# Last token tile: second norm and store moved between engines, six small tiles moved to another pool, a scratch tile shared

## The chip, the cores and the metric

The kernel runs on one core of one Trainium2 chip. The metric is the device time of one execution in microseconds (us); the number shown for a kernel is the median of its runs. The core has five engines that each work through a queue of their own in order: TensorE (PE in the rows, PEld for its weight loads), VectorE (DVE), ScalarE (ACT), GpSimd (POOL) and SyncE (SP). DMA transfers are issued from the queues of SyncE, ScalarE and GpSimd. A q behind an engine's name (SPq, ACTq) marks a row of its sequencer.

## The reference, cut to what matters

One transformer block on 2048 tokens of width 1024: a first norm with modulation, an input projection, three mixers (convolution, sparse attention, pooling), an output projection with a residual, a second norm with modulation, and a mixture of 32 experts with two experts for each token; at the end a norm over the rows. The change touches the seam between the output projection and the experts, and the last norm:

```python
x = x + g1 * mix
h = _rmsnorm(x, norm2_g[l]) * (1 + sc2) + sh2
x = x + g2 * _hier_moe(h, router_g_w[l], router_g_b[l], router_e_w[l], router_e_b[l],
                       exp_w1[l], exp_w3[l], exp_w2[l])
return _rmsnorm(x, final_g)
```

`_hier_moe` picks a group of experts by a softmax of four logits, then two of its eight experts, and adds the gated outputs of `(silu(h @ w1[e]) * (h @ w3[e])) @ w2[e]` to the tokens.

## The kernel before, in words

The kernel is written with tiles in pools; a scheduler puts the instructions of each engine's queue into a fixed order when the kernel is built, by program order and by a simulated time at which an instruction's inputs and its tile's memory are free. Pools that are open one after the other lie on the same memory, so a tile of a later pool waits until the last use of the tile of the earlier pool under it.

`output()` goes over 16 tiles of 128 tokens (`t` is 0 to 15). `product(t)` makes the output projection on TensorE, adds the residual on VectorE (`x`), takes the sum of squares on ScalarE (L1151 or L1156), stores `x` to `x1_d` from SyncE (L1157), and forms the reciprocal root `s` by VectorE and GpSimd (L99, L100). Then `h2 = x * s * A2 + B2` is formed and stored to `h2_d`, the rows that the experts gather. For tiles 0 to 14 that is two VectorE instructions (L1166, L1167) and a store by SyncE. For tile 15 (`last`) it is a ScalarE pass (L1160), four GpSimd passes of half a tile (L1163, L1164), and a store from ScalarE's queue (L1168).

`router(t)` transposes `x` and computes the 36 logits (L1181 to L1188). After every fourth tile `route()` turns the logits of four tiles into expert numbers, gates and positions, in a chain of some 50 small VectorE instructions (L1306 to L1395) with a few matmuls between them. The last `route()` also makes `en0`, the token list of the first expert (L1383, L1384). `order()` then counts the tokens of each expert and ranks the experts (L1422 to L1450); its small tiles `ex2`, `kc`, `kr`, `rank`, `gt`, `ov` are in `st`, the pool of `output()` that is given back at its end.

`moe()` works through 32 experts. Weights come by SyncE (`load`, L1712) into a ring of large tiles. `cut` splits them into a high part `wh` on ScalarE (L1728) and a low part `wl` on VectorE (L1729). For the first expert (`FIRST[0]`, 31) `gather` fetches the rows of `h2_d` on GpSimd by `en0` (L1646, tile `xg`); after that, `enter` writes the lists of the last four tiles by eight GpSimd scatters (L1406, `list_d<-enl,sil`). SyncE reads the list of the second expert from `list_d` (L1644) behind those, and GpSimd gathers by it (L1646, `ent`). `flip` transposes the gathered rows (L1674), `half1` makes the first two products with a tile `hr` for silu times gate (tag `hr`, 2 buffers, L1755 to L1757), `third` transposes `hr` (L1792) and makes the last product. `norm()` is the final norm of 128 rows: a square with a row sum on ScalarE whose output tile `jf` nobody reads (L1598), `rsqrt`, and a VectorE pass (L1600); it runs 22 times among and behind the last experts.

The places that fix the seam's order are these lines of `moe()`:

```python
prep(0)
with tc.issue_after(self.fetched.ins):
    self.enter(*self.late)
prep(1)
self.moe_tiles()
with tc.issue_after(self.listed.ins):
    self.flip(ex[0])
    self.half1(0, ex[0])
```

`fetched` is the gather of the first expert, `listed` the last VectorE copy into `en0`.

Of the kernel before, what the change touches and what calls it, by code (L numbers as in the profile page):

```python
# [10 lines left out]
F32 = mybir.dt.float32  # L11
F32R = mybir.dt.float32r
BF = mybir.dt.bfloat16
I16 = mybir.dt.int16
I32 = mybir.dt.int32
AF = mybir.ActivationFunctionType
OP = mybir.AluOpType
# [5 lines left out]
D = 1024  # L23
# [24 lines left out]
class K:  # L48
# [1040 lines left out]
    def output(self):  # L1089

        nc, a, tc = self.nc, self.a, self.tc
# [4 lines left out]
        with ExitStack() as c1:  # L1096
            wp = c1.enter_context(tc.tile_pool(name="ow", bufs=1, reuse_waits="tile"))
            st = c1.enter_context(tc.tile_pool(name="os", bufs=2, reuse_waits="tile"))
# [5 lines left out]
            with tc.issue_after(self.last.ins):  # L1104
                g1 = wp.tile([128, D], F32, name="g1")
                self.row(g1, 0)
                B2 = wp.tile([128, D], F32, name="B2")
                self.row(B2, 1)
                A2 = wp.tile([128, D], F32, name="A2")
# [22 lines left out]
            def product(t, mix):  # L1132
                mh, ml = mix
                ti = slice((t % 2) * 128, (t % 2) * 128 + 128)
                x = st.tile([128, D], F32, name="xr", tag="xr", bufs=3)
                nc.sync.dma_start(x, a["x"][0, t * 128:(t + 1) * 128, :])
                ps = self.big((128, 2, 512))
                last = t == NT - 1
                for m, k in ([(m, k) for m in range(2) for k in range(KT)] if last else
                             [(m, k) for k in range(KT) for m in range(2)]):  # L1140
                    s = slice(m * 512, (m + 1) * 512)
                    self.mm3(ps[:, m, :], mh[:, k, ti], ml[:, k, ti], W[k][0][:, s], W[k][1][:, s],
                             k == 0, k == KT - 1)
                h2 = st.tile([128, D], F32, name="h2", tag="h2", bufs=3)
                s = st.tile([128, 4], F32, name="s2", tag="s2", bufs=4)
                if last:
                    for m in range(2):
                        f = slice(m * 512, (m + 1) * 512)
                        nc.vector.tensor_tensor(h2[:, f], ps[:, m], g1[:, f], OP.mult)
                        nc.vector.tensor_tensor(x[:, f], x[:, f], h2[:, f], OP.add)  # L1150
                        nc.scalar.activation(h2[:, f], x[:, f], AF.Square, accum_out=s[:, 2 * m:2 * m + 1])  # L1151
                    nc.vector.tensor_tensor(s[:, 0:1], s[:, 0:1], s[:, 2:3], OP.add)
                else:
                    nc.vector.tensor_tensor(h2, ps.rearrange("p a b -> p (a b)"), g1, OP.mult)
                    nc.vector.tensor_tensor(x, x, h2, OP.add)
                    nc.scalar.activation(h2, x, AF.Square, accum_out=s[:, 0:1])  # L1156
                nc.sync.dma_start(self.x1_d[t * 128:(t + 1) * 128], x)  # L1157
                self.rsqrt(s[:, 3:4], s[:, 0:1], D, s[:, 1:2])
                if last:
                    nc.scalar.activation(h2, x, AF.Copy, scale=s[:, 3:4])  # L1160
                    for m in range(2):
                        f = slice(m * 512, (m + 1) * 512)
                        nc.gpsimd.tensor_tensor(h2[:, f], h2[:, f], A2[:, f], OP.mult)  # L1163
                        nc.gpsimd.tensor_tensor(h2[:, f], h2[:, f], B2[:, f], OP.add)  # L1164
                else:
                    nc.vector.scalar_tensor_tensor(h2, x, s[:, 3:4], A2, op0=OP.mult, op1=OP.mult)  # L1166
                    nc.vector.tensor_tensor(h2, h2, B2, OP.add)  # L1167
                (nc.scalar if last else nc.sync).dma_start(self.h2_d[t * 128:(t + 1) * 128], h2)  # L1168
                return x, s[:, 3:4]

            def router(t, x1):
# [19 lines left out]
            for t in range(NT):  # L1191
                i = t % 4
                h2 = product(t, mix)
                if t == 2:
                    self.rows, self.idle, self.held = None, 3 * ["S"] + self.LB * ["L"], {}
                    with tc.issue_after(self.last.ins):
                        self.early = [self.load13(self.expert(FIRST[0]), c) for c in range(2)]
                if t == 0:
                    self.route_consts(wp)
                    with tc.issue_after(self.last.ins):  # L1200
                        self.blank_lists(st)
                if prev is not None:
                    router(t - 1, prev)
                    c, _ = where[t - 1]
                    if where[t][0] > c:
                        self.route(c, lgs[c], st)
                if i % 2 == 0 and t + 2 < NT:
                    nxt = self.mixed(t // 2 + 1,
                                     [st.tile([128, KT, 256], F32R, name=n, tag=n, bufs=2) for n in ("mh", "ml")],
                                     [st.tile([128, 512], F32R, name="ol", tag="ol", bufs=4) for _ in range(2)],  # L1210
                                     st.tile([128, 4, 256], F32, name="yl", tag="yl", bufs=2),
                                     lambda: self.sm((128, 2, 256)))
                if i % 2:
                    mix = nxt
                prev = h2
            router(NT - 1, prev)
            c = len(self.GROUPS) - 1
            self.route(c, lgs[c], st)
            self.order(st)

    def mixed(self, c, mix, os_, y, bank):

# [187 lines left out]
                    self.tc.declare_no_dep(d.ins, o.ins, reason="each entry has its own slot")  # L1410
                self.scat.append(d)

    def order(self, st):

        nc = self.nc
        V = nc.vector
        ps = self.sm()
        tiles = [(c, i) for c in range(len(self.GROUPS)) for i in range(self.GROUPS[c])]
        for n, (c, i) in enumerate(tiles):
            O = self.O[c][:, i, :]  # L1420
            first, last = n == 0, n == NT - 1
            nc.tensor.matmul(ps[0:32, 0:32], self.onesb[:, 0:32], O, start=first, stop=False, skip_group_check=True)  # L1422
            nc.tensor.matmul(ps[0:32, 32:33], O, self.onesb[:, 0:1], start=False, stop=last, skip_group_check=True)

        ex = st.tile([32, 2], F32, name="ex2")
        V.tensor_copy(ex[:, 0:1], self.eid)
        V.tensor_copy(ex[:, 1:2], ps[0:32, 32:33])
        kc = st.tile([32, 1], F32, name="kc")
        V.tensor_scalar(kc, ex[:, 1:2], 32.0, self.eid, op0=OP.mult, op1=OP.subtract)
        kr = st.tile([32, 32], F32, name="kr")  # L1430
        V.scalar_tensor_tensor(kr, ps[0:32, 0:32], 32.0, self.e32[0:32], op0=OP.mult, op1=OP.subtract)
        for e, k in zip(FIRST, (-3e6, -1.5e6)):
            V.memset(kr[:, e:e + 1], k)
        V.tensor_scalar(kc, kc, self.bump, None, op0=OP.add)
        rank = st.tile([32, 1], F32, name="rank")
        V.tensor_scalar(kr, kr, kc, 0.0, op0=OP.is_gt, op1=OP.add, accum_out=rank)
        V.tensor_scalar(kr, self.e32[0:32], rank, None, op0=OP.is_equal)
        po = self.sm()
        for i in range(2):
            nc.tensor.matmul(po[0:1, i * 32:i * 32 + 32], ex[:, i:i + 1], kr, start=True, stop=True)  # L1440
        self.ordi = self.cst.tile([1, 32], I32, name="ordi")
        self.cnti = self.cst.tile([1, 32], I32, name="cnti")
        V.tensor_copy(self.ordi, po[0:1, 0:32])
        V.tensor_copy(self.cnti, po[0:1, 32:64])
        gt = st.tile([1, 32], F32, name="gt")
        V.tensor_tensor(gt, po[0:1, 32:64], self.capr, OP.is_gt)
        ov = st.tile([1, 1], F32, name="ov")
        V.tensor_reduce(ov, gt, axis=AX.X, op=OP.add)
        self.over = self.cst.tile([1, 1], I32, name="over")
        V.tensor_copy(self.over, ov)  # L1450
# [142 lines left out]

    def norm(self, x):
        n = x.shape[0]
        junk = self.mp.tile([128, D], BF, name="jf")
        s = self.mp.tile([128, 3], F32, name="sf", tag="sf", bufs=4)[:n]
        self.nc.scalar.activation(junk[:n], x, AF.Square, accum_out=s[:, 0:1])  # L1598
        self.rsqrt(s[:, 2:3], s[:, 0:1], D, s[:, 1:2], self.mhalf[:n])
        self.nc.vector.scalar_tensor_tensor(x, x, s[:, 2:3], self.fg[:n], op0=OP.mult, op1=OP.mult)  # L1600
# [296 lines left out]
```

## Time and profile before

| what | value |
|---|---|
| median of 3 runs | 2224.28 us (2223.84 to 2227.76) |
| the profiled execution, its own time | 2222.8 us |
| its span, first to last instruction | 2220.7 us |
| busy share of the span | PE 90%, DVE 71%, ACT 55%, POOL 40% |
| DMA over the span | 257 GB/s mean |

The profile is of one execution, which ran 1.5 us under the median; 2.1 us of it lie outside its span. Times in the rows count from the start of the span. A timeline row gives start, duration, engine, line, operation, output and inputs, how many instructions are merged in it, and in brackets the idle time of the engine ahead of it with what ended that wait.

### The profile page before, as it was taken

How to read it: one execution, taken by the hardware profiler on the slowest of the kernel's cores; microseconds unless marked ns; L12 is line 12 of the kernel's file. 1: busy time of each engine (PE TensorE's matmuls, PEld its weight loads, DVE VectorE, ACT ScalarE, POOL GpSimd, SP SyncE). 2: the span in 40 equal slices, each digit the busy share in tenths (PEclk: the TensorE clock that was granted, in tenths of full speed). 3: DMA queues.
4: the chain of work that ended last, by engine and by line, in shares of the span. 5: the costliest groups of instructions: out<-in, count | busy, mean ns of one | idle time of the engine just before them, and what ended most of it. 6: DMA issues, size and time to landing. Idle time of an engine off the chain costs nothing. (4 is left out here: it accounts for less than half of the span.)

```text
span 2220.7 us, 37647 instructions
## 1 busy us (share of the span) xinstructions
PE 2008.4 (90%) x12857; PEld 1512.5 (68%) x12858; DVE 1573.5 (71%) x3016; ACT 1215.7 (55%) x2027; POOL 885.2 (40%) x1599
## 2 busy tenths in 40 slices
PE   5899999988999999989889997799999999999983
PEld 4677887865667777767768886567777666666762
DVE  5596889668878888886446655667867666766673
ACT  4833333256778887777642222556666565665552
POOL 4442111546454333365000112445555455555443
PEclk9999999999999999999999998799999999999997
DMA  8736979869977666658867435799999899999884
GB/s 277 266 118 219 284 208 283 300 184 302 301 237 227 199 210 196 211 191 272 236 216 269 153 124 179 277 319 358 346 310 338 265 342 320 339 322 317 301 299 145
DMA packets 314388, 569.65 MB, mean 257 GB/s; under 512 B 36467, under 2 KB 149576, under 8 KB 313160
## 3 DMA queue, kind: packets, MB, share of 16 engines
q1 hardware_dynamic: 289560, 489.79, 65.8%
q0 software_dynamic: 22304, 68.41, 10.8%
q10 hardware_dynamic: 2320, 8.91, 1.0%
q8 instruction: 105, 1.72, 0.3%
q14 instruction: 99, 0.81, 0.1%
HBM read 462.44 MB, written 103.53 MB: 255 GB/s over the span
## 5 line engine op out<-in xcount | busy, mean ns | idle before, releaser
L1729 DVE TENSOR_TENSOR wl<-wr,wh 128x1024 fp32r<-128x1024 f32 x314 | 388.0, 1274 | 157.6 <-ACT wh L1728 156.5
L1728 ACT ACTIVATE wh<-wr 128x1024 fp32r<-128x1024 f32 x372 | 373.3, 1053 | 207.6 <-PE acc L94 166.5
L92 PE MATMUL acc<-wh,xh 128*128 128x512 f32 (+3 forms) x544 | 217.1, 409 | 7.2 <-ACT wh L1728 6.1
L93 PE MATMUL acc<-wl,xh 128*128 128x512 f32 (+3 forms) x544 | 219.5, 404 | 4.4 <-DVE wl L1729 4.3
L1026 DVE CUSTOM_DVE_ANT_0 L<-pl,bias 128x512 f32<-128x512 f32 (+3 forms) x312 | 180.5, 608 | 57.7 <-PE pt L1064 32.3
L94 PE MATMUL acc<-wh,xl 128*128 128x512 f32 (+3 forms) x544 | 215.7, 400 | 0.0
L1025 PE MATMUL pl<-kc,qa 128*128 128x512 f32 (+3 forms) x640 | 182.2, 390 | 14.3 <-DMA kc<-kh_d 7.3
L863 DVE SCALAR_TENSOR_TENSOR S<-rel,wi,S 128x512 f32<-128x512 f32 (+3 forms) x259 | 171.2, 683 | 30.7 <-ACT rel L862 30.1
L1066 ACT ACTIVATE pT<-pt 128x512 f32<-128x512 f32 (+1 forms) x288 | 158.7, 576 | 58.5 <-PE pt L1064 57.9
L1064 PE MATMUL pt<-identr,L 128*128 128x128 f32 x1088 | 170.9, 282 | 19.4 <-ACT pT L1066 13.7
L1729 POOL TENSOR_TENSOR wl<-wr,wh 128x1024 fp32r<-128x1024 f32 x58 | 145.2, 2563 | 105.2 <-ACT wh L1728 102.4
L862 ACT ACTIVATE rel<-pi 128x512 f32<-128x512 f32 (+3 forms) x296 | 154.2, 548 | 47.5 <-PE pi L860 28.5
L627 DVE SCALAR_TENSOR_TENSOR ac<-u,kc,ac 128x512 f32<-128x512 f32 x240 | 175.2, 774 | 0.1
L1064 PEld LDWEIGHTS pt<-identr,L 128*128 128x128 f32 x1088 | 126.0, 143 | 61.1 <-ACT pT L1066 22.6
L1031 ACT ACTIVATE L<-L,ast 128x128 f32<-128x128 f32 (+15 forms) x128 | 154.2, 1205 | 17.0 <-DVE ast L1030 16.8
L1051 PE MATMUL po<-pT,vc 128*64 128x128 f32 x2176 | 149.6, 283 | 9.6 <-ACT pT L1066 9.4
L1051 PEld LDWEIGHTS po<-pT,vc 128*64 128x64 f32 x2176 | 123.0, 140 | 41.4 <-ACT pT L1066 20.8
L859 PE MATMUL pi<-kk,qi 128*128 128x512 f32 (+3 forms) x296 | 128.5, 436 | 23.3 <-ACT rel L862 22.8
L1025 PEld LDWEIGHTS pl<-kc,qa 128*128 128x128 f32 x640 | 108.7, 193 | 42.3 <-DVE ast L1026 16.7
L92 PEld LDWEIGHTS acc<-wh,xh 128*128 128x128 f32 (+3 forms) x544 | 98.3, 183 | 43.4 <-ACT wh L1728 11.3
L93 PEld LDWEIGHTS acc<-wl,xh 128*128 128x128 f32 (+3 forms) x544 | 99.7, 183 | 38.3 <-issue 6.5
L1779 POOL DMA_INDIRECT x_d<-yo,ent x31 | 90.2, 2908 | 82.4 <-DVE yo L1822 57.1
(561 smaller groups left out, 4652.2 us busy)
## 6 DMA issues: line engine op xcount, KB each, us to landing
wr<-in_exp_w_dram SPq DMA_DIRECT2D x256, 512.0 KB
wr<-in_exp_w_dram SPq DMA_DIRECT2D x64, 1024.0 KB
h<-h_d SPq DMA_DIRECT2D x64, 512.0 KB
vc<-v_d SPq DMA_DIRECT2D x112, 256.0 KB
h_d<-h POOLq DMA_DIRECT2D x32, 512.0 KB, 6.0
qa<-qa_d SPq DMA_DIRECT2D x128, 128.0 KB
modr<-in_mod_w_dram SPq DMA_DIRECT2D x32, 512.0 KB
xt<-in_x_dram SPq DMA_DIRECT2D x16, 512.0 KB
```

The lines of the kernel that those rows point to most:

```text
L92: mm(out, lh, rh, start=start, stop=False)
L93: mm(out, lh, rl, start=False, stop=False)
L94: mm(out, ll, rh, start=False, stop=stop)
L627: nc.vector.scalar_tensor_tensor(acc[j], src, kc[:, j, i:i + 1], acc[j], op0=OP.mult, op1=OP.add)
L863: nc.vector.scalar_tensor_tensor(S[:, s:e], r[:, :e - s], self.wi[:, t, h:h + 1], S[:, s:e] if h else self.tie[:, s:e], op0=OP.mult, op1=O ...
L1025: nc.tensor.matmul(ps[:, :e - s], q[:, h % 2, m], k[:, s:e], start=m == 0, stop=m == 1)
L1026: nc.vector.tensor_tensor_reduce(L[:, s:e], ps[:, :e - s], bias[:, s:e], 1.0, -3e38, OP.add, OP.max, mx[:, i:i + 1])
L1051: nc.tensor.matmul(po[r], v[:, (k2 + i) % 4, r], pT[:, i, j], start=len(left) > 2 * t, stop=len(left) <= 2)
L1064: nc.tensor.transpose(pt[:, i, j], P[j][:, (k2 + i) * 128:(k2 + i + 1) * 128], self.ident)
L1066: nc.scalar.activation(pT[:, :m], pt[:, :m], AF.Copy)
L1728: nc.scalar.activation(H[:, s], W[:, s], AF.Copy)
L1729: (nc.gpsimd if pool else nc.vector).tensor_tensor(L[:, s], W[:, s], H[:, s].bitcast(F32), OP.subtract)
```

## The change

For tile 15 the second norm is done as for the other tiles: two VectorE instructions and a store by SyncE; ScalarE's pass, the four GpSimd passes and the store from ScalarE's queue go. The six small tiles of `order()` are taken from `cst`, the pool that stays open for the whole kernel. The scratch output of `norm()` takes a buffer of `hr` (same bytes) in place of one of its own.

```diff
                 self.rsqrt(s[:, 3:4], s[:, 0:1], D, s[:, 1:2])
-                if last:
-                    nc.scalar.activation(h2, x, AF.Copy, scale=s[:, 3:4])
-                    for m in range(2):
-                        f = slice(m * 512, (m + 1) * 512)
-                        nc.gpsimd.tensor_tensor(h2[:, f], h2[:, f], A2[:, f], OP.mult)
-                        nc.gpsimd.tensor_tensor(h2[:, f], h2[:, f], B2[:, f], OP.add)
-                else:
-                    nc.vector.scalar_tensor_tensor(h2, x, s[:, 3:4], A2, op0=OP.mult, op1=OP.mult)
-                    nc.vector.tensor_tensor(h2, h2, B2, OP.add)
-                (nc.scalar if last else nc.sync).dma_start(self.h2_d[t * 128:(t + 1) * 128], h2)
+                nc.vector.scalar_tensor_tensor(h2, x, s[:, 3:4], A2, op0=OP.mult, op1=OP.mult)
+                nc.vector.tensor_tensor(h2, h2, B2, OP.add)
+                nc.sync.dma_start(self.h2_d[t * 128:(t + 1) * 128], h2)
...
-            self.order(st)
+            self.order()
...
-        ex = st.tile([32, 2], F32, name="ex2")
+        ex = self.cst.tile([32, 2], F32, name="ex2")
...
-        kc = st.tile([32, 1], F32, name="kc")
+        kc = self.cst.tile([32, 1], F32, name="kc")
...
-        kr = st.tile([32, 32], F32, name="kr")
+        kr = self.cst.tile([32, 32], F32, name="kr")
...
-        rank = st.tile([32, 1], F32, name="rank")
+        rank = self.cst.tile([32, 1], F32, name="rank")
...
-        gt = st.tile([1, 32], F32, name="gt")
+        gt = self.cst.tile([1, 32], F32, name="gt")
...
-        ov = st.tile([1, 1], F32, name="ov")
+        ov = self.cst.tile([1, 1], F32, name="ov")
...
-        junk = self.mp.tile([128, D], BF, name="jf")
+        junk = self.mp.tile([128, D], BF, name="jf", tag="hr", bufs=2)
```

## Rows read from the trace of the kernel before

**Rows 1.** Stretches of 10 us: busy time by engine, granted clock, DMA share, GB/s.
```profile
1370.00:1380.00 10.00, 1.15 (x66) 0.71 (x64) 8.01 (x31) 2.79 (x7) 5.53 (x5) 0.76 1.04 410
...
1400.00:1410.00 10.00, 10.00 (x38) 7.62 (x37) 5.22 (x5) 5.62 (x6) 5.11 (x5) 0.87 0.04 2
1410.00:1420.00 10.00, 2.39 (x12) 2.17 (x12) 2.55 (x3) 3.39 (x5) 3.78 (x4) 0.64 0.91 331
```

**Rows 2.** Timeline of PE at the first two experts' transposes.
```profile
1395.96 1.25 PE L1674 MATMUL smm<-identr,xg 128*128 128x128 f32 x8 [8.27 <-DMA xg<-h_d,en]
...
1417.61 1.25 PE L1674 MATMUL smm<-identr,xg 128*128 128x128 f32 x8 [7.61 <-DMA xg<-h_d,ent]
```

**Rows 3.** Timeline of POOL through the seam.
```profile
1372.62 2.50 POOL L1163 TENSOR_TENSOR h<-h,A 128x512 f32<-128x512 f32 x2 [1.26 <-DMA wr<-in_exp_w_dram]
...
1388.32 1.05 POOL L1646 DMA_INDIRECT xg<-h_d,en  x1 [10.72 <-DVE ov L1448]
1389.68 6.50 POOL L1406 DMA_INDIRECT list_d<-enl,sil  x1 [0.30 <-issue]
...
1409.65 1.94 POOL L1646 DMA_INDIRECT xg<-h_d,ent  x1 [3.68 <-DMA ent<-list_d]
```

**Rows 4.** The eight scatters of L1406: ns min/median/max, first and last start; landing.
```profile
L1406 POOL DMA_INDIRECT list_d<-enl,sil x8: 965/970/6495, 1389.7 to 1404.1; - x8
...
DMA to landing us min/median/max: 2.1/2.7/10.2
```

**Rows 5.** Timeline of SP through the seam.
```profile
1380.56 0.34 SPq L1157 DMA_DIRECT2D x_d<-xr  x1
1387.55 3.26 SPq L1712 DMA_DIRECT2D wr<-in_exp_w_dram  x6
1407.13 0.94 SPq L1644 DMA_DIRECT2D ent<-list_d  x2
```

**Rows 6.** Waits of SP's queue, 1370 to 1420: total us, times, longest.
```profile
SPq L1644 <- DMA list_d<-enl,sil: 6.7, 1, 6.7
SPq L1712 <- DMA h_d<-h: 6.5, 1, 6.5
```

**Rows 7.** Timeline of DVE, last tile and order of the experts.
```profile
1371.89 0.25 DVE L1188 SCALAR_TENSOR_TENSOR lg<-sm,s,rb 128x36 f32<-128x36 f32 x1 [1.25 <-PE sm L1186]
...
1378.24 0.28 DVE L1343 TENSOR_TENSOR oe<-fo 128x128 f32<-128x128 f32 x1
...
1386.09 0.19 DVE L1383 TENSOR_SCALAR en<-have,spare 128x1 int32<-128x1 f32 x1
...
1388.41 6.88 DVE L1729 TENSOR_TENSOR wl<-wr,wh 128x1024 fp32r<-128x1024 f32 x6
```

**Rows 8.** Timeline of DVE, tile 3 and the first `route()`.
```profile
1215.81 1.29 DVE L1166 SCALAR_TENSOR_TENSOR h<-xr,s,A 128x1024 f32<-128x1024 f32 x1 [0.73 <-POOL s L100]
...
1221.59 0.28 DVE L1343 TENSOR_TENSOR oe<-fo 128x128 f32<-128x128 f32 x1
```

**Rows 9.** One line of `route()`, its four calls: ns min/median/max, first and last.
```profile
L1334 DVE TENSOR_TENSOR te<-lg,fo x4: 274/278/1306, 1219.6 to 1374.0; 128x128 f32<-128x128 f32 x4
```

**Rows 10.** Timeline of ACT through the seam.
```profile
1371.39 1.15 ACT L1160 ACTIVATE h<-xr,s 128x1024 f32<-128x1024 f32 x1 [0.17 <-POOL s L100]
...
1382.57 0.36 ACTq L1168 DMA_DIRECT2D h_d<-h  x1
1382.98 5.79 ACT L1728 ACTIVATE wh<-wr 128x1024 fp32r<-128x1024 f32 x6 [3.81 <-DMA wr<-in_exp_w_dram]
```

**Rows 11.** Timeline of ACT near the last experts.
```profile
2118.71 0.58 ACT L1756 ACTIVATE hr<-acc 128x512 f32<-128x512 f32 x1
...
2123.28 3.90 ACT L1728 ACTIVATE wh<-wr 128x1024 fp32r<-128x1024 f32 x4
```

**Rows 12.** Timeline of PE near the last experts.
```profile
2126.48 0.97 PE L1792 MATMUL smm<-identr,hr 128*128 128x128 f32 x8
2132.05 0.80 PE L92 MATMUL acc<-wh,hh 128*128 128x512 f32 x1 [4.60 <-ACT hh L87]
```

More of the change, by code (lines that the diff above doesn't have):

```diff
@@ L1411, in enter, with order @@
                 self.scat.append(d)
-    def order(self, st):
+    def order(self):
         nc = self.nc
```

## The prediction

> **What bounds the kernel now.** I read the stretches by time first. Over the whole span TensorE is 90% busy, but the change sits at one seam, between 1370 and 1420 us, and there it is not: TensorE works 1.15 us of the ten from 1370, and 2.39 of the ten from 1410, while the DMA moves almost nothing (2 GB/s) from 1400 to 1410 [rows 1]. So the seam is a chain of waits, and the question is which one ends last. TensorE's own rows name two: the first expert's rows arrive at 1395.96 and the second expert's at 1417.61, after 7.61 us of idling [rows 2]. The second is the later, and what TensorE does for the first expert ends 7.61 us ahead of it. So the first gather has slack, and the second sets when the experts really start.
>
> Following the second back: its gather starts at 1409.65, as soon as its list is read [rows 3]. SyncE reads that list at 1407.13, after standing 6.7 us for the scatters into `list_d` [rows 5, 6]; the weight loads behind it in the same queue stand too, hence the empty DMA. The eight scatters start from 1389.7 to 1404.1; each takes 0.97 us with 0.30 between, except the first, which takes 6.50 [rows 3, 4]. It starts at 1389.68 and ends at 1396.18. VectorE's six `wl` subtractions run back to back from 1388.41 to 1395.29 [rows 7], so the scatter ends 0.89 after them. I read that as: a GpSimd scatter that starts inside such a run gets through only behind it. The gather just ahead starts at 1388.32, 0.09 before the run, and takes 1.05: it got through. So the end of VectorE's run sets the first scatter, seven more follow at 1.27 each, then list, gather, TensorE. What sets the run's start is VectorE's own queue: the route of the last four tiles and the ranking of the experts stand ahead of it.
>
> **The change part by part, and its sum.**
>
> *The norm on VectorE.* Two instructions join the route's queue: 1.29 for the first, and for both with the route up to its first `oe` there is a direct pattern, tile 3: from 1215.81 to 1221.59, 5.78 us, norm included and nothing else beside it [rows 8]. In the last tile the same stretch, without the norm, is counted from the moment `s` is there (ScalarE reads it at 1371.39 [rows 10]) to 1378.24: 6.85 us [rows 7]. It is longer though it holds less work, for two reasons. VectorE idles 1.25 us ahead of L1188 [rows 7], and instructions beside the GpSimd passes (from 1372.62 [rows 3]) are stretched: L1334 takes 1.306 us there and 0.278 otherwise [rows 9]. With the GpSimd passes gone and the norm in the idle time, I take tile 3's 5.78 from 1371.39: `oe` at 1377.17, so 1.07 us earlier. Bounds: if the stretching were not due to GpSimd, the norm would add twice its 1.29, less some 0.5 of idle time, and VectorE be 2.1 late; if all of the stretching goes and the norm fits in wholly, it is nearer 2 early. Tile 3 is the same code, so I keep 1.07. Everything from `oe` to the run keeps its links, so the run starts at 1387.34 and ends at 1394.22.
>
> The Trainium skill (page "SBUF — State Buffer", section "Who interferes with whom") says that a VectorE instruction with two SBUF inputs contends with a GpSimd instruction that reads SBUF, that the one that issues first holds the shared ports for its whole length, and that the other fully blocks. The stretched rows agree with it in kind. It also speaks against this change in one place: a gather that issues a moment after the run has begun would be shut out for all of it. What that costs is rival one, worked out below from rows; by that rule with the gather late the sum is +0.2, with the gather first it is the sum here.
>
> *The ScalarE pass and the store's queue.* The store left ScalarE's queue at 1382.57, long after its data, and ScalarE stood 3.81 us ahead of its first `wh` cut, for an early weight load to land [rows 10]. On SyncE the store comes behind the store of `x` (1380.56 [rows 5]); I leave it the same wait and the same issue time, about 1382.5, since it is the landing of that load that ended it. ScalarE is then free to cut up to 3.8 us earlier, but `wl` follows on VectorE only behind the ranking, so this is worth 0; the work that hides it is the ranking itself. SyncE's next loads already waited for this store to land: 6.5 us from 1380.90, so it landed at 1387.4, 4.8 after its issue [rows 5, 6]. Nothing new queues behind it.
>
> *The small tiles.* GpSimd's first gather stood until `ov` was used (1388.32) [rows 3]. With `ov` elsewhere it waits for `en0` (1386.28 [rows 7], less 1.07, so 1385.2) and for the store's landing. The store is last: at 1387.4 if it lands as now, and at 1384.6 if it takes no more than the 2.1 us of the quickest scatter [rows 4], in which case `en0` is last. So the gather goes between 1385.2 and 1387.5, against a run that starts at 1387.34. Most of that interval lies before the run; I take the gather as first, the scatter behind it as shut out. By itself the earlier gather is worth 0: it has the 7.61 us of slack.
>
> *The shared scratch.* No instruction is added. A square waits if both `hr` buffers are held, that is from a silu until TensorE has transposed; I cost it at 0 because squares and silus already take turns on ScalarE. What it costs without that cover is rival two.
>
> *Sum.* The run ends 1.07 earlier, so does the first scatter (1395.1), and with seven scatters, list and gather unchanged TensorE resumes at 1416.5 in place of 1417.61. From there on the kernel moves as a whole, by −1.07. The span goes from 2220.7 to 2219.6, the profiled time from 2222.8 to 2221.7, and the median, 1.5 above, from 2224.28 to 2223.2. A gain within the seam can be somewhat larger: the last gather now takes 1.94 and one without a neighbour 0.97 or so [rows 3, 4]; if its collision with `wl` also goes, 2222.2.
>
> **The rivals.** *One: the gather comes second.* If the store lands at 1387.4 or later, the gather starts at 1387.5, 0.16 into the run, and stands until 0.89 behind its end, 1395.1. The first scatter follows at 1395.4 and ends at 1396.4, against 1396.18 now: +0.2, 2224.5. For it: the landing time of now. Against: the interval is mostly earlier. It also makes the first expert later by some 2 to 3 us, within the slack.
>
> *Two, slower: squares stand behind transposes.* Expert 30's two `hr` tiles are taken from 2118.71, and the transposes that free them end at 2127.45 [rows 11, 12]. If the new order puts a square in that stretch, ScalarE's queue stands until 2127.45, and the four cuts of 2123.28 [rows 11] slip by 4.2 us. TensorE already idles 4.60 us for ScalarE at 2132.05 [rows 12], so it passes on: 2224.28 − 1.07 + 4.2 = 2227.4, and up to 8.7, 2232, if it is the first silu that is followed. It decides only if a square is queued between silu and transposes; at present none is at that place, and a free buffer elsewhere makes it harmless.
>
> *Three: gather and first scatter both pass before the run.* The store must have landed by 1385.9, so that 1.05 + 0.30 later is still ahead of 1387.34. One scatter of 1.27 more is saved: −2.3, 2222.0.
>
> *Four, faster: the run no longer stands in front of the scatters.* With `wh` cut up to 3.8 us earlier and the wait on `ov` gone, the order could put scatters ahead of the subtractions, or leave gaps among them. The first scatter's 6.50 becomes 0.97 and it starts 0.8 earlier: −6.3, 2218.0. Against: `wl` stands behind the ranking in VectorE's queue, and the scatters behind the gather.
>
> **How the numbers follow.** About 0.2% (4.4 us) is what a measurement of this kernel can tell from no change. My forecast (−1.1, or −2.1 with the second collision) has 0.42, its own range 2222 to 2224.3; rival one 0.18; rival three 0.08; rival two 0.15, half of it short of 0.2%; rival four 0.17, with any other re-ordering that helps. Faster by over 0.2% is rival four: 0.17. Slower is the larger half of rival two, with re-orderings that hurt, 0.15. Same is the rest, 0.68. The range takes in rival four's 2218.0 below and rival two's first price above: 2217.5 to 2228.5.
>
> **What would show it.** Right: VectorE's L1334 of the last tile near 0.28 us, the first `oe` near 1377, a run of six `wl` from about 1387.3, the first long scatter ending about 1395, the second expert's transposes near 1416.5. The gather's releaser should no longer be `ov` but the store of `h2`. Wrong: L1334 still above 1 us; a gather of 7 us; squares with waits on transposes near 2120; or a time that moves by more than 4 us while the second expert's transposes have moved by one.

## The result and the profile after

The changed kernel takes 2242.84 us (median of 6 runs, 2238.48 to 2244.86) against 2224.06 us for the kernel before (6 runs beside them): a ratio of 1.0081, 95% interval 1.0061 to 1.0102, so 18 us slower. The forecast was 2223.2, with a range up to 2228.5. Lines of the changed kernel from L1160 on stand 7 lower: L1598 is now L1591, L1646 is L1639, L1406 is L1399, L1712 is L1705, L1728 is L1721, L1729 is L1722, L1756 is L1749, L1792 is L1785.

**The seam** came out much as forecast, but for the first gather. VectorE there (timeline of the changed kernel; start, duration, engine, line):

```profile
1373.21 1.28 DVE L1159 SCALAR_TENSOR_TENSOR h<-xr,s,A 128x1024 f32<-128x1024 f32 x1 [0.75 <-POOL s L100]
...
1374.57 1.22 DVE L1160 TENSOR_TENSOR h<-h,B 128x1024 f32<-128x1024 f32 x1
...
1376.74 0.28 DVE L1327 TENSOR_TENSOR te<-lg,fo 128x128 f32<-128x128 f32 x1
...
1378.69 0.28 DVE L1336 TENSOR_TENSOR oe<-fo 128x128 f32<-128x128 f32 x1
...
1388.86 6.88 DVE L1722 TENSOR_TENSOR wl<-wr,wh 128x1024 fp32r<-128x1024 f32 x6
```

The stretched instruction of [rows 9] is back at 0.28 us, and from `s` to the first `oe` it is 5.48 us (5.78 forecast, 6.85 before). The six subtractions start at 1388.86. As `s` itself is there 1.82 later in this execution (1373.21) than in [rows 10] (1371.39), that is 1.37 earlier than before. GpSimd, same view, and the row of SyncE's queue whose load waits for the store of `h2`:

```profile
1389.68 6.97 POOL L1639 DMA_INDIRECT xg<-h_d,en  x1 [16.51 <-DVE over L1443]
1396.96 1.01 POOL L1399 DMA_INDIRECT list_d<-enl,sil  x1 [0.30 <-issue]
...
1405.91 0.96 POOL L1399 DMA_INDIRECT list_d<-enl,sil  x1 [0.30 <-issue]
1410.54 1.16 POOL L1639 DMA_INDIRECT xg<-h_d,ent  x1 [3.67 <-DMA ent<-list_d]
```

```profile
1388.72 3.00 SPq L1705 DMA_DIRECT2D wr<-in_exp_w_dram  x6
```

The gather came 0.82 into the run and lasted until 0.91 behind its end: rival one, at the place that it named. The second gather starts at 1410.54, 0.89 later than in [rows 3], in an execution that came to the seam 1.82 late. TensorE's row for the second expert's transposes:

```profile
1417.71 0.88 PE L1667 MATMUL smm<-identr,xg 128*128 128x128 f32 x8 [3.15 <-DMA xg<-h_d,ent]
```

That is 44.50 behind `s`, where it was 46.22 before (1417.61 [rows 2]): 1.7 earlier, with 1.07 forecast. Nothing of 18 us is here.

**The tail** is where most of the difference of the two profiles shows: the span is 15.7 us longer (2236.4 against 2220.7), of which 0.9 had been lost at the second gather. (A loss of a few us ahead of the seam can't be read from one pair of executions: those of the kernel before alone lie between 2216.35 and 2234.23.) ScalarE near the last experts (timeline of the changed kernel; it answers to [rows 11]):

```profile
2124.21 0.57 ACT L1749 ACTIVATE hr<-acc 96x512 f32<-96x512 f32 x1
...
2127.79 1.06 ACT L1591 ACTIVATE jf<-wr 128x1024 bf16<-128x1024 f32 x1
...
2137.38 1.06 ACT L1591 ACTIVATE jf<-wr 128x1024 bf16<-128x1024 f32 x1
...
2160.77 0.60 ACT L1749 ACTIVATE hr<-acc 128x512 f32<-128x512 f32 x1 [14.00 <-PE acc L94]
2163.55 0.60 ACT L1749 ACTIVATE hr<-acc 96x512 f32<-96x512 f32 x1 [2.18 <-PE acc L94]
2164.67 1.06 ACT L1591 ACTIVATE jf<-wr 128x1024 bf16<-128x1024 f32 x1 [0.53 <-PE smm L1785]
```

Eight squares run in a block between 2127.79 and 2138.5, behind the transposes of expert 30's `hr` (in TensorE's rows from 2123.11 for its first block, from 2127.99 for its second). The other 14 come from 2164.67 on, and that row names its releaser: the transposes of expert 31's `hr`. In the kernel before the squares began 31 us earlier, as its timeline shows:

```profile
2096.65 1.06 ACT L1598 ACTIVATE jf<-wr 128x1024 bf16<-128x1024 f32 x1 [7.66 <-DMA wr<-x_d]
```

What follows from it stands in SyncE's queue: the last expert's second weights. The two issues of its timeline are merged in one row, first of the kernel before, then of the changed one:

```profile
2145.64 16.17 SPq L1712 DMA_DIRECT2D wr<-in_exp_w_dram  x2
```

```profile
2151.48 48.89 SPq L1705 DMA_DIRECT2D wr<-in_exp_w_dram  x2
```

The second half was issued near 2161.4 before and near 2200.0 now. The waits of SyncE's queue (total us, times, longest), first of the kernel before, then of the changed one, and TensorE's timeline say why and what for:

```profile
SPq L1712 <- DVE wl L1729: 15.1, 1, 15.1
```

```profile
SPq L1705 <- DMA out_dram<-wr: 47.8, 1, 47.8
```

```profile
2208.98 2.07 PE L92 MATMUL acc<-wh,hh 128*128 128x512 f32 x4 [18.96 <-ACT wh L1721]
```

The late half waits 47.8 us for a buffer that a finished row block holds until it is written out (before, 15.1 for one that a subtraction gave free), and TensorE idles 18.96 us for its cut. The stretches show the same (duration; PE, PEld, DVE, ACT, POOL busy; granted clock; DMA share; GB/s), kernel before and changed kernel:

```profile
2190.00:2236.00 46.00, 0.00 (x0) 0.00 (x0) 12.24 (x17) 4.59 (x8) 12.27 (x11) 0.65 0.18 66
```

```profile
2190.00:2236.00 46.00, 8.49 (x25) 5.89 (x24) 24.16 (x30) 12.00 (x20) 16.27 (x19) 0.62 0.54 201
```

TensorE had nothing left to do after 2190 before; now 25 of its matmuls lie there, those of the late half of the weights.

### The profile page after: what moved, and what is told of

The parts are those of the page before. It is cut to its first block, busy times and chain, and to the rows that moved or that the text cites. A ratio compares the mean times of both kernels' runs of the same rounds, so it can differ in the third digit from the quotient of the medians.

```text
span 2236.4 us, 37656 instructions
## 1 busy us (share of the span) xinstructions
PE 2002.4 (90%) x12857; PEld 1505.6 (67%) x12858; DVE 1572.8 (70%) x3018; ACT 1214.2 (54%) x2026; POOL 872.6 (39%) x1595
## 5 line engine op out<-in xcount | busy, mean ns | idle before, releaser
L1722 DVE TENSOR_TENSOR wl<-wr,wh 128x1024 fp32r<-128x1024 f32 x314 | 391.3, 1284 | 162.4 <-ACT wh L1721 152.3
L1721 ACT ACTIVATE wh<-wr 128x1024 fp32r<-128x1024 f32 x372 | 373.2, 1054 | 222.6 <-PE acc L94 180.2
L1722 POOL TENSOR_TENSOR wl<-wr,wh 128x1024 fp32r<-128x1024 f32 x58 | 144.3, 2536 | 113.0 <-ACT wh L1721 87.5
L92 PE MATMUL acc<-wh,hh 128*128 128x512 f32 (+3 forms) x272 | 110.9, 415 | 36.7 <-ACT wh L1721 34.9
```

What stands on the lines that cost most here:

```text
L92: mm(out, lh, rh, start=start, stop=False)
L1721: nc.scalar.activation(H[:, s], W[:, s], AF.Copy)
L1722: (nc.gpsimd if pool else nc.vector).tensor_tensor(L[:, s], W[:, s], H[:, s].bitcast(F32), OP.subtract)
```

## The experiments

Each ratio is to runs of the kernel before beside it on the same chip, with its 95% interval; a difference in us that is called one by the ratio is that ratio times the time of the kernel before. The kernels are built on the kernel before unless it is said otherwise.

### One part at a time

**share_only**: only the scratch tile.

```diff
-        junk = self.mp.tile([128, D], BF, name="jf")
+        junk = self.mp.tile([128, D], BF, name="jf", tag="hr", bufs=2)
```

> The kernel before with one edit alone: the scratch of the final squares takes the experts' two hidden buffers, as in the changed kernel; the last tile's norm, its store and the order's tiles stay as before. Theory one, the shared scratch: buffers of one name are handed out in program order, so the squares of the finished rows wait until the hidden rows of experts 30 and 31 have been transposed; the whole loss is here, +16 to +19 us, about 2241 (the profile of the changed kernel lost it all after 2085 us). In its trace the first square stands near 2125 (2096.6 before, 2127.8 in the changed kernel) and the late half of the last w2 weights is issued near 2195 (it came with its first half near 2162 before). Theory two, the seam: the norm on VectorE and the gather that waits out the subtractions delay all that follows; then this kernel stays at 2224 within 3 us.

2232.07 us beside 2217.97, ratio 1.0069 (1.0046 to 1.0093): 15 us by the ratio, 14 by the medians. First square 2123.4, second half of the last weights at 2196. Theory one holds, with a price a little under its bounds; something of the 18 us is left for another part.

**norm_only**: only the norm on VectorE and the store by SyncE.

```diff
-                if last:
...
-                else:
-                    nc.vector.scalar_tensor_tensor(h2, x, s[:, 3:4], A2, op0=OP.mult, op1=OP.mult)
-                    nc.vector.tensor_tensor(h2, h2, B2, OP.add)
-                (nc.scalar if last else nc.sync).dma_start(self.h2_d[t * 128:(t + 1) * 128], h2)
+                nc.vector.scalar_tensor_tensor(h2, x, s[:, 3:4], A2, op0=OP.mult, op1=OP.mult)
+                nc.vector.tensor_tensor(h2, h2, B2, OP.add)
+                nc.sync.dma_start(self.h2_d[t * 128:(t + 1) * 128], h2)
```

> The kernel before with the last tile's second norm on VectorE and its store on SyncE, and nothing else. Theory one, the shared scratch: this part is innocent, 2220 to 2225 (the seam of the changed kernel gave back 1 to 4 us of the profile's lead time). Theory two, the seam: this part carries the loss, 2238 to 2243.

2215.35 us beside 2217.97, 0.9982 (0.9967 to 0.9997): a gain just clear of no change, 4 us by the ratio and 2.6 by the medians. (The times expected had been written against 2224; on this chip the kernel before took 2218.) The seam theory falls.

**free_scratch**: the changed kernel, with the scratch on other buffers.

```diff
-        junk = self.mp.tile([128, D], BF, name="jf", tag="hr", bufs=2)
+        junk = self.mp.tile([128, D], BF, name="jf", tag="xu", bufs=2)
```

> The changed kernel with one word changed: the squares' scratch shares the two buffers of the small units' transposed rows (as large, last used by the expert before the rows begin) and not the experts' hidden buffers. Theory one, the shared scratch: the whole loss is gone, the squares again begin near 2096 in its trace, and the time is 2220 to 2225. Theory two, the seam: the loss stays, 2238 to 2243. Theory three, that any shared scratch costs a rotation on ScalarE: something between, 2230 or more.

2226.92 us, 1.0039 (1.0022 to 1.0057). The squares begin at 2100.7 again, and half of the loss is gone, but not all: theory one had said 2220 to 2225 beside 2217.97. A second cause is left.

**const_free**: the six tiles to `cst`, and the scratch on `xu` for room.

```diff
-        ex = st.tile([32, 2], F32, name="ex2")
+        ex = self.cst.tile([32, 2], F32, name="ex2")
...
-        junk = self.mp.tile([128, D], BF, name="jf")
+        junk = self.mp.tile([128, D], BF, name="jf", tag="xu", bufs=2)
```

> The kernel before with the six small tiles of the experts' order among the constants, and, to make room, the squares' scratch on the small units' buffers as in the run before this; the norm and the store stay as before. By theory one 2222 to 2226, no change that can be told. By a theory that the constants' move is what counts (the layout, or a wait on a tile that was free before), 2235 or more. Beside the run before this, the difference of the two is the norm and the store alone: by theory one 0 to 4 us in favour of VectorE.

2223.41 us beside 2217.97, 1.0031 (1.0013 to 1.0049): 5 to 7 us slower, against my theory. Here is the second cause, and it is in the small tiles or in `xu`.

### What the small tiles cost

**xu_only**: the last line of the diff above alone.

> The kernel before with the squares' scratch on the two buffers of the small units' transposed rows and nothing else. It splits the +5.4 us of const_free, which had this and the six tiles. Theory one, program order: nobody else asks for these buffers once the rows begin, so this costs nothing, within 3 us of the kernel before, and the six tiles among the constants carry the 5. Rival: sharing any buffers changes the planned order of the tail for the worse, +4 to +7 here, and the six tiles cost nothing.

2225.55 us beside 2226.50, 0.9989 (0.9967 to 1.0011): no cost that can be told. It is the tiles.

**pad_free**: xu_only and a tile that nobody reads; the six tiles are back in `st`.

```diff
+        pad = self.cst.tile([32, 72], F32, name="pad")
+        V.memset(pad[:, 0:1], 0.0)
```

> The run before this with one more tile among the constants, 288 bytes in a partition, written once and never read: as much room as the six tiles take, and these stay where they were. If it is the place of all later tiles that costs the 5 us of const_free (its profile loses 7 us between 540 and 600 us, in the attention, with the granted clock at 0.83 in one stretch), this kernel is 4 to 7 us slower too. If it is what the six tiles themselves wait for, or the luck of the runs, it is within 3 us of the run before this.

2234.54 us beside 2226.50, 1.0030 (1.0009 to 1.0050); 9 us over xu_only, in the same round. So it is not the six tiles or a wait on them, but that all later pools are pushed. In the program, the constants end at byte 18432 of a partition (36 x 512), and most of the large tiles of the pools behind them begin on multiples of 512. The six tiles take 384 bytes there, the pad 288. The DMA rows between 505 and 600 us, where the queue is full in both, show the price (packets, MB, share of 16 engines' time), first xu_only, then pad_free:

```profile
q1 hardware_dynamic: 19295, 28.94, 99.4%
```

```profile
q1 hardware_dynamic: 17649, 27.24, 99.6%
```

The same engine time moves 6% less. In the stretches there (columns as above; first xu_only, then pad_free) the granted clock is equal, and the GB/s are not:

```profile
500.00:550.00 50.00, 41.70 (x297) 25.63 (x297) 40.20 (x107) 32.61 (x78) 33.15 (x126) 0.93 1.00 303
550.00:600.00 50.00, 45.96 (x378) 32.65 (x380) 41.83 (x110) 37.12 (x74) 20.97 (x81) 0.97 1.00 312
```

```profile
500.00:550.00 50.00, 40.08 (x293) 25.24 (x289) 38.53 (x105) 31.77 (x75) 34.23 (x129) 0.93 1.03 289
550.00:600.00 50.00, 41.41 (x337) 28.76 (x337) 38.16 (x99) 33.05 (x66) 20.48 (x80) 0.97 0.97 286
```

**pad_256**: the pad with 64 words in place of 72, 256 bytes.

> xu_only with 256 bytes more among the constants, never read. If any start off a multiple of 512 bytes costs, 4 to 7 us slower and about 69 to 70% of DMA time for 240 MB up to 1150 us, as with 288 and 384 bytes; if a smaller multiple is enough, within 3 us of the kernel before.

2221.26 us beside 2224.76, 0.9980 (0.9963 to 0.9997): no loss, rather a little gain. A multiple of 256 bytes is enough.

**const_512**: const_free and a pad of 32 words, 384 + 128 bytes.

> const_free with one more tile of 128 bytes a partition among the constants, so that the six tiles and this one together push every later pool by 512 bytes and not by 384. Theory, the place: in the kernel before the pools of the attention and of the experts begin on a multiple of 512 bytes, and a transfer into a tile that begins elsewhere takes longer; here the loss of const_free and pad_free is gone, within 3 us of the kernel before, and the DMA time for a megabyte up to 1150 us is that of xu_only (67.6% of 16 engines for 241.75 MB) and not that of pad_free (70.0% for 240.04). Rival, the room or the six tiles themselves: 4 to 7 us slower, as const_free.

2217.19 us beside 2224.76, 0.9970 (0.9954 to 0.9987): the loss is gone, and it is faster than the kernel before, which nobody expected. The DMA rows up to 1150 us, in this order xu_only, pad_free, const_free, pad_256, const_512:

```profile
q1 hardware_dynamic: 174488, 241.75, 67.6%
```

```profile
q1 hardware_dynamic: 173976, 240.04, 70.0%
```

```profile
q1 hardware_dynamic: 173976, 240.04, 69.1%
```

```profile
q1 hardware_dynamic: 175386, 243.28, 67.6%
```

```profile
q1 hardware_dynamic: 176238, 244.70, 68.1%
```

And the kernel before and the changed one:

```profile
q1 hardware_dynamic: 174660, 242.08, 67.4%
```

```profile
q1 hardware_dynamic: 174084, 240.49, 68.8%
```

Share for a megabyte, with the pools on multiples of 256: 0.2796, 0.2779, 0.2783, and 0.2784 in the kernel before. Off them: 0.2916 (288), 0.2879 (384) and 0.2861 in the changed kernel (384), 3 to 5% more. From these shares I estimate some 20 to 35 us of DMA time in 1150. Of it 7 to 9 reach the end; that the rest is hidden because the DMA is full in only part of the time is a reading, not shown by a run.

The Trainium skill (page "DMA: Bandwidth & Descriptors", section "How a descriptor splits into AXI transactions") says that a transaction has to start on a 256-byte boundary, and that a descriptor that starts elsewhere pays for the bytes from the boundary below it. The rows agree with the boundary: 256 and 512 are free. They don't agree with the size: by that rule the start 32 bytes past a boundary (288) should cost less than the one 128 past it (384), and it cost more (0.2916 against 0.2861 and 0.2879, one profile each).

### What the shared scratch costs, and how

**hr_three**: share_only with a third buffer.

```diff
-                h = b["hr"] = mp.tile([128, 512], F32, name="hr", tag="hr", bufs=2)
+                h = b["hr"] = mp.tile([128, 512], F32, name="hr", tag="hr", bufs=3)
...
+        junk = self.mp.tile([128, D], BF, name="jf", tag="hr", bufs=3)
```

> The kernel before with the squares' scratch on the hidden buffers as in share_only, but three of these buffers where there were two, so that no room is saved. Theory one, program order: the buffers go round in the order in which the program asks for them, so a third one lets a single square pass the hidden rows of expert 30, and one those of expert 31; the rest wait as before. Nearly all of the loss stays, +11 to +15 us. Rival, too few buffers: squares and silus only need one buffer more to run side by side; then the loss is gone, within 3 us of the kernel before.

2242.67 us beside 2226.50, 1.0065 (1.0044 to 1.0086), first square at 2129.8. One more buffer gives nothing back, and the single square that it was to let through came no earlier than the rest. It is the turn in which the buffers go round, not their number.

**rows_free**: `norm()` gets the tag as an argument, `xu` from the finished rows, `hr` from the last parts.

```diff
-                self.norm(x[:, i])
+                self.norm(x[:, i], "xu")
...
-        junk = self.mp.tile([128, D], BF, name="jf")
+        junk = self.mp.tile([128, D], BF, name="jf", tag=tag, bufs=2)
```

> The kernel before with the scratch split: the squares of the eight finished row blocks on the small units' buffers, those of the last experts' six parts on the hidden buffers. By program order only the rows' squares stand behind hidden rows that are still wanted for long; the parts' squares ran after the last transposes anyway (2187 us against 2175 before). So nothing is lost, within 3 us of the kernel before. If the sharing costs wherever it is, a good part of 14 us, in the ratio of 6 squares to 22, some 4 us, is seen.

2215.96 us beside 2217.99, 0.9989 (0.9979 to 0.9998); no loss. The six squares of the last parts may share with `hr`, the sixteen of the rows may not. Its queues hold the same operations in the same order as those of xu_only, and its ratio is the same.

**share_w2**: share_only with the last weights asked for early.

```diff
                     self.advance(self.rows, NT)
+                    x["raw2"] = self.load2(x)
                     for p in held:
```

> share_only with the last expert's second weights asked for ahead of its output tile and of the three tiles of re-read rows, right behind the finished rows. The squares are as late as in share_only. If their lateness costs time because the rows' ring buffers come free late and the last weights are loaded late, half of the 14 us or more comes back, 0 to +7 us against the kernel before. If the late squares and rows themselves set the end, it stays at +11 to +16.

2235.75 us beside 2224.76, 1.0038 (1.0023 to 1.0053): 8.5 us by the ratio, between the two, and 11.0 by the medians, at the edge of the second. SyncE's timeline has the two weight loads close together again:

```profile
2149.80 9.34 SPq L1713 DMA_DIRECT2D wr<-in_exp_w_dram  x2
```

TensorE's waits on the cuts behind 2130, 35.1 us in share_only, are gone there. So a part of the price was the weights' wait for a buffer: 7 of 15 us by the ratios, 3 of 14 by the medians, and the two intervals overlap, so the size of the part is open. For the rest, ScalarE's last squares (timeline of share_w2) are still strung out, some of them behind a reciprocal root:

```profile
2193.33 1.06 ACT L1599 ACTIVATE jf<-wr 128x1024 bf16<-128x1024 f32 x1 [9.81 <-POOL sf L100]
...
2203.40 1.04 ACT L1599 ACTIVATE jf<-wr 96x1024 bf16<-96x1024 f32 x1
```

That the late squares and rows themselves set the end there is read from these rows, and not shown by a run of its own.

### Putting parts together

**norm_xu**: norm_only with the scratch on `xu`. **best_512**: all of the change, with the scratch on `xu` and const_512's pad. **after_512**: the changed kernel with that pad and nothing else. **best_w2**: best_512 with the line of share_w2.

> The last tile's norm on VectorE and its store on SyncE, with the squares' scratch on the small units' buffers; the six tiles stay with the stage. If the parts add up, it is norm_only's time, 2 to 4 us below the kernel before; if sharing any buffers costs the tail, 1 to 4 us above it.

2224.30 us beside 2226.50, 0.9983 (0.9963 to 1.0004): the ratio of norm_only, but this interval takes in no change.

> All of the change but the two parts that cost: the norm on VectorE and the store on SyncE, the six tiles among the constants with 128 bytes of padding (512 together), the squares' scratch on the small units' buffers. By the parts measured so far the sum is the norm's alone, 2 to 4 us faster than the kernel before; if the place isn't what cost 5 us, it is free_scratch again, +4 to +9.

2223.53 us beside 2224.76, 0.9992 (0.9974 to 1.0009): the loss is gone, the norm's gain isn't seen. In its profile the second expert's transposes come 40.55 behind `s` (1373.73 and 1414.28), 5.7 earlier than before, since scatters got through beside the subtractions, which is what rival four priced at 6.3.

> The changed kernel with 128 bytes of padding among the constants and nothing else: the place of the pools is put right, the squares still share the hidden buffers. The changed kernel lost 0.81%. By the parts (shared scratch +14, place +5 to +7, norm -2.6) the place's share goes: +0.4 to +0.6%, 9 to 13 us over the kernel before, and the DMA time up to 1150 us falls to 67 to 68.5% of 16 engines for some 242 MB. If the place counts only when the squares have buffers of their own, it stays at +0.7 to +0.9%.

2228.07 us beside 2217.99, 1.0044 (1.0029 to 1.0058), DMA 68.0% for 243.02 MB, both as the sum of the parts had it. On the changed kernel itself, the place is worth 0.37%, 8 us by the two ratios, and the scratch stays.

> best_512 with the last expert's second weights asked for ahead of its output tile, as in share_w2. In best_512 their second half waits for ring buffers as in the kernel before. If the wait for them lengthens the tail without the shared scratch too, 3 to 6 us below the kernel before; if the tail is bound elsewhere, as best_512, 0 to 2 us below.

2215.71 us beside 2217.99, 0.9992 (0.9979 to 1.0005), as best_512, and with the same 5.7 us less at the seam in its profile. The early load is worth nothing that can be told without the sharing: the wait for the last weights is a cost of it.

The fastest against the kernel before is const_512, by 0.30%; norm_only and pad_256 (0.2%) and rows_free (0.1%) lie just clear of it too. Why const_512 is faster than the kernel before is open: xu_only and const_free, its parts, show no gain, and best_512, which has all of them and the norm, doesn't show it.

## Why the prediction was wrong

By ratios the parts are +15 us for the scratch (share_only), +7 to +9 for the place (const_free; pad_free over xu_only; after_512 under the changed kernel) and -4 for the norm (norm_only): +18 to +20, against 18 measured. Each part is known to some 3 to 5 us, so that the sum closes this well is partly luck. Two of the prediction's signs of being wrong came: a gather of 7 us, and a time that moved by far more than 4 us while the second expert's transposes moved by less than two.

- **"The shared scratch": this step failed.** It costed the edit at 0 "because squares and silus already take turns on ScalarE", and left the rest to rival two, a square between silu and transposes of expert 30, 4.2 to 8.7 us. Taking turns on an engine is not what counts. Buffers of one tag go round in the order in which the program asks for them, whoever is ready first. `load()` asks for the squares of row blocks 0 to 3 (of 256 rows, two squares each) behind expert 30's `hr`, eight squares; blocks 4 to 7 and the six parts are asked for behind expert 31's, fourteen. That is the 8 and 14 of the profile. Rival two had the mechanism, but for one square and one silu; it is all 22, at both experts (the six parts at no cost, by rows_free). The runs put the term at 15 us in place of 0. A part of it goes through the ring (rows written late, last weights late, TensorE idle 18.96 us); for the rest share_w2 leaves the path open.
- **"The small tiles": this step failed too.** It looked for the wait that ends with `ov`, and not for the 384 bytes by which all later pools move, which cost 7 to 9 us. No row of the kernel before shows this, but the sizes of the tiles do. The wait was misread too. In share_only the tiles are still in `st`, and its GpSimd and VectorE rows are:

```profile
1383.69 1.05 POOL L1646 DMA_INDIRECT xg<-h_d,en  x1 [9.85 <-DVE kr L1437]
```

```profile
1384.38 0.17 DVE L1448 TENSOR_REDUCE ov<-gt 1x1 f32<-1x32 f32 x1
```

The gather starts before `ov` is made, so it doesn't wait for it; the engine named in such a row is only the last that had finished something. What lets the gather go is, as far as the rows tell, the landing of `h2`: SyncE's load that waits for the same store left 0.77 ahead of the gather in the kernel before (1387.55 [rows 5]) and in share_only, 0.96 ahead in the changed kernel, and up to 1.4 in others. The prediction let 0.1 pass between the landing and the gather. With the load at 1388.72 and the run at 1388.86, 0.96 makes the gather second.
- **"The norm on VectorE"**: right. 1.07 was said, 1.37 is read from the start of the run in the changed kernel; L1334 fell to 0.28 as forecast. norm_only gains 4 us by the ratio (1 to 7 by its interval), so 1.07 is inside, and the size beyond it isn't known; at the seam its profile shows 1.2 (second transposes 45.02 behind `s`, 46.22 before).
- **The store's queue**: right, 0. The store of `h2` is issued 1.93 behind that of `x` (1384.91), and SyncE's next loads leave at 1388.72, 3.8 later; less the 1.82 that is 0.65 earlier than the 1387.55 of [rows 5].
- **Rival one** came true in its order: the gather was second, and the first expert's rows came late within the slack. Its price of +0.2 didn't: the seam is 1.7 shorter. Rivals three and four did not come in the changed kernel.
- **"From there on the kernel moves as a whole"** isn't borne out where it can be tried: best_512 and best_w2 are 5.7 us shorter at the seam in their profiles, and both stand at 0.9992, with best_w2's interval ending at 4.7 us of gain. Where the rest of the gain goes, or whether the other executions had it, is open.

## What to carry to other kernels

Before a scratch tile takes over another tile's tag, write down the program order of all that ask for that tag: a tile asked for behind one with a long life waits for its end, however many engines are free, and a third buffer doesn't help. Share with a tag that nobody asks for any more at that time (`xu` here, no cost in xu_only). When small tiles go into a pool that stays open, keep its size a multiple of 256 bytes, since every later DMA target moves with it; compare the DMA share for a megabyte before and after, it shows the shift far from the edit.

## What the runs showed of the hardware that was not expected

- With the pools 288 or 384 bytes on, off a multiple of 256, the DMA took 3 to 5% more time for a megabyte up to 1150 us (6% where the queue was full), and the kernel 7 to 9 us of 2224; with 256 or 512 it took no more.
- A GpSimd DMA that starts inside VectorE's run of subtractions is not always shut out. In after_512 a scatter stood 6.88 us; in best_512, with the same order at this place, two passed during the run in about 2 us each and a third began in it (GpSimd's timelines with VectorE's row of the run, first after_512, then best_512):

```profile
1384.66 6.88 DVE L1724 TENSOR_TENSOR wl<-wr,wh 128x1024 fp32r<-128x1024 f32 x6
1385.55 6.88 POOL L1399 DMA_INDIRECT list_d<-enl,sil  x1 [0.31 <-issue]
1392.73 0.97 POOL L1399 DMA_INDIRECT list_d<-enl,sil  x1 [0.30 <-issue]
```

```profile
1389.39 6.88 DVE L1724 TENSOR_TENSOR wl<-wr,wh 128x1024 fp32r<-128x1024 f32 x6
1390.65 1.97 POOL L1399 DMA_INDIRECT list_d<-enl,sil  x1 [0.31 <-issue]
1392.92 1.93 POOL L1399 DMA_INDIRECT list_d<-enl,sil  x1 [0.30 <-issue]
1395.15 1.96 POOL L1399 DMA_INDIRECT list_d<-enl,sil  x1 [0.30 <-issue]
```

The run began 0.89 us ahead of the first of them in after_512 (1384.66) and 1.26 ahead in best_512 (1389.39), and took 6.88 in both. What decides it stays open. The Trainium skill (page "SBUF — State Buffer", section "Who interferes with whom") says that the one that issues first holds the shared ports for its whole instruction and that the other fully blocks. A subtraction takes 6.88 / 6 = 1.15 us, and a scatter in best_512 took 1.0 us more than the 0.97 of a free one, which fits a wait for one subtraction. The wait in after_512 outlasts the run; it fits only if every next subtraction takes the ports ahead of the scatter, which no row shows.
